# Attention's decay summed by a scan on VectorE instead of products with a triangle, and the convolution's first output ahead, in a two-layer hybrid trunk

## The chip, the cores and the metric

The kernel runs on one core of a Trainium2 chip. The metric is the device time of one execution in microseconds; the median of the runs stands for the kernel. Of an execution taken by the profiler there are also the span (first to last instruction) and a trace of every engine: TensorE (PE, its weight loads PEld), VectorE (DVE), ScalarE (ACT), GpSimd (POOL) and SyncE's queue of DMA issues (SPq).

## The reference

A trunk of two layers on 512 tokens of width 1024. Each layer has a SwiGLU feed-forward block (inner width 2816) at half weight, a mixer, and a second such block, each behind an RMSNorm. The mixer projects the normalised input once and splits the columns over three groups: a causal convolution of width 3, HGRN2 (a gated linear recurrence, 4 heads), and FoX, attention with a forget gate (8 heads). What the change touches is FoX's decay and the convolution:

```python
def short_conv_mixer(x_in, b_gate, c_gate, conv_w):
    u = c_gate * x_in
    ...                       # y = causal depthwise convolution of u, width 3
    return b_gate * y

def fox_mixer(q, k, v, f_logit, f_bias, q_gain, k_gain):
    ...
    log_f = jax.nn.log_sigmoid((f_logit + f_bias).astype(f32))
    cum = jnp.cumsum(log_f, axis=1).transpose(0, 2, 1)
    ...
        s = (jnp.einsum('bhqd,bhkd->bhqk', qb, kh).astype(f32)
             + (cb[..., :, None] - cum[..., None, :]))
        s = jnp.where(qpos[:, None] >= kpos[None, :], s, MASK_VALUE)
        p = jax.nn.softmax(s, axis=-1)
```

`cum` is the running sum of the gates' logarithms over the 512 tokens, for each of 8 heads.

## The kernel before, in words

Activations lie with features on the 128 partitions and the 512 tokens along the row. Almost all products are float32 split into a rounded part and a rest, three products for one (`mm3`, lines 496, 502 and 503, or line 582 where `stream_steps` writes the order of the rests out, `lows`). Weights come by DMA from SyncE's queue into a stage tile `st` (L417), ScalarE copies the rounded part into a tile `hl` (L477), and VectorE subtracts it to get the rest (L483). `stream_steps` goes through a projection in granules of `kk` blocks of 128 rows; a granule has a list `order` of (output bank, block), three products each. It is block by block, with the output banks in turn, except where `lead` is set in the first granule, or in the last granule: there it is bank by bank.

PSUM has eight banks with names that go round: three `mm`, two `sc`, two `pt`, one `po`.

In a mixer (`mix`) the order is this. First come HGRN's projections and the tokens' gates, the FoX forget logits `zf` among them (128 partitions x 4 blocks of tokens x 8 heads). Then two generators `run`, one for each pair of HGRN heads, are stepped beside `dense`, FoX's projections (`fox_qkv`: q and k of four heads twice, and the values, each with four output banks `mm`, `mm`, `mm`, `po`). HGRN's tensors of 128x512 are taken from a pool of ten tiles `t`. In a step of `run` the state is summed by a scan on VectorE (L1636), the operands of levels 0 and 1 are made (L1654 to L1659), and the scores of these levels are taken on TensorE (L1676); the operands of the later levels follow (L1665 to L1668) with their scores (L1686).

`fox_decay` is called between these steps, once in a layer, after the operands of levels 0 and 1. It makes the logarithms `lf` (128 x 4 x 8) and sums them over the tokens: it splits `lf` into a rounded part `lh` and a rest `ll` (L1803, L1804), and for each block j of 128 tokens multiplies both by `utri`, a constant of 128x512 whose first 128 columns are an upper triangle of ones and whose others are all ones (L1808, eight products of 512, 384, 256 and 128 columns). The sum stands in a `pt` bank as 8 heads x 512 tokens. ScalarE writes its negative, rounded, to `negc` (L1812), VectorE the rest (L1813), and SyncE sends both to device memory (L1818), from where the attention's preparation of each head reads them (L1904). The constant is built once in the opening (`build_consts`, L355 to L358).

After `dense` comes `conv`, run beside the attention's steps (`BESIDE`). It makes two projections of two outputs each (`features_steps`, granules of four blocks, `deep=4`), with output banks `mm`, and then a third. The banks that the first of them takes are those that held the values' projection, which ScalarE and VectorE clear (L1884, L1885).

Instructions are put in order on each engine by a planner with modelled durations, with the program's order as priority; chains written out by hand (`follow`, `keep`) fix the order of TensorE's products in `conv`, in attention and in `dense`.

Of the kernel before, what the change touches and what calls it, by code (L numbers as in the profile page):

```python
# [8 lines left out]
F32 = mybir.dt.float32  # L9
F32R = mybir.dt.float32r  # L10
# [3 lines left out]
AF = mybir.ActivationFunctionType  # L14
ALU = mybir.AluOpType
# [13 lines left out]
P = 128  # L29
T = 512  # L30
# [54 lines left out]
NH = 8  # L85
C_X, C_B, C_C, H_Q, H_F, H_I, H_G = (256 * i for i in range(7))
# [130 lines left out]
def halves(x):  # L217

    return x.rearrange("p (h t) -> p h t", h=2)


def unwoven(bank):

    return bank.rearrange("p (t h) -> p h t", h=2)
# [12 lines left out]
def inner(x):  # L237

    return x.rearrange("p (b t h) -> p b h t", h=2, t=CH)
# [12 lines left out]
class Trunk:  # L252
# [40 lines left out]
    def build_consts(self, scratch):  # L293

        nc = self.nc
        c = self.const

        self.ones_blk = c.tile([P, P], F32R, tag="ones_blk", name="ones_blk")
        nc.vector.memset(self.ones_blk.bitcast(F32), 0.0)
        for h in range(2):  # L300
            r = slice(64 * h, 64 * h + 64)
            nc.vector.memset(self.ones_blk[r, r].bitcast(F32), 1.0 / 64)

        self.heads2 = c.tile([P, 2], F32, tag="heads2", name="heads2")
        nc.vector.memset(self.heads2, 0.0)
        for h in range(2):
            nc.vector.memset(self.heads2[64 * h : 64 * h + 64, h : h + 1], 1.0)

        self.smask = c.tile([P, T], F32, tag="smask", name="smask")
        nc.vector.memset(self.smask, 1.0)  # L310
        nc.vector.memset(self.smask.rearrange("p (c t) -> p c t", t=CH)[:, :, 0:1], 0.0)
        self.identb = c.tile([P, P], BF16, tag="identb", name="identb")
        nc.vector.tensor_copy(self.identb, self.ident)
        self.utri = c.tile([P, T], F32R, tag="utri", name="utri")
        self.maskb = c.tile([P, P], BF16, tag="maskb", name="maskb")

        self.lmask = c.tile([P, 6, CH], U8, tag="lmask", name="lmask")
        self.same = c.tile([P, CH], F32, tag="same", name="same")
        ft = scratch(I32)[:, :P]
        pt = scratch(I32)[:, :P]  # L320
        nc.gpsimd.iota(ft, pattern=[[1, P]], base=0, channel_multiplier=0)
        nc.gpsimd.iota(pt, pattern=[[0, P]], base=0, channel_multiplier=1)
        ftf = scratch(F32)[:, :P]
        ptf = scratch(F32)[:, :P]
        x = scratch(I32)[:, :P]
        for i in (
            nc.vector.tensor_copy(ftf, ft), nc.vector.tensor_copy(ptf, pt),
            nc.vector.tensor_tensor(x, ft, pt, op=ALU.bitwise_xor),
        ):
            self.tc.add_manual_dep(i.ins, self.first_rows, NOSYNC, reason="opening order")  # L330
        xf = scratch(F32)[:, :CH]
        later = scratch(F32)[:, : P + CH]
        later, own = later[:, :P], later[:, P:]
        nc.vector.tensor_tensor(later, ftf, ptf, op=ALU.is_gt)
        for h in range(2):

            r = slice(CH * h, CH * h + CH)
            nc.vector.tensor_copy(xf[r], x[r, r])
            nc.vector.tensor_copy(own[r], later[r, r])
            nc.vector.tensor_copy(self.same[r], self.ident[r, r])  # L340
        a = scratch(F32)[:, :CH]
        b = scratch(F32)[:, :CH]
        for l in range(1, 7):
            nc.vector.tensor_scalar(
                a, xf, scalar1=float(2 ** (l - 1)), scalar2=None, op0=ALU.is_ge
            )
            nc.vector.tensor_scalar(b, xf, scalar1=float(2**l), scalar2=None, op0=ALU.is_lt)
            nc.vector.tensor_mul(a, a, b)
            nc.vector.tensor_mul(self.lmask[:, l - 1, :], a, own)

        nc.vector.tensor_scalar(
            inner(self.maskb)[:, 0], halves(later), scalar1=-1e30, scalar2=None, op0=ALU.mult
        )

        nc.vector.tensor_tensor(self.utri[:, :P], ftf, ptf, op=ALU.is_ge)  # L355
        of = scratch(F32)[:, P:]
        nc.vector.memset(of, 1.0)
        nc.vector.tensor_copy(self.utri[:, P:], of)  # L358

    def n(self, s):  # L360
        self.uid += 1
# [955 lines left out]
    def mix(self, l, w, w_out, conv_w, out_gain, q_gain, k_gain, f_bias, next_gain, logits):  # L1317
        nc, tc = self.nc, self.tc
        FM2 = [slice(0, P), slice(P, 2 * P)]
        TOK = [slice(c, c + P) for c in (0, 128, 256, 384)]  # L1320
        with tc.tile_pool(name=self.n("mix"), bufs=1) as mp:
# [23 lines left out]
            def features_steps(spans, banks, mid=None, **kw):  # L1345

                bs = [self.bank(t) for t in banks]
                yield from self.stream_steps(
                    [(b, c, None) for b, c in zip(bs, FM2)], cols(*spans), self.xact, KD, mid, **kw
                )  # L1350
                return bs
# [18 lines left out]
            with tc.tile_pool(name=self.n("hg"), bufs=1) as hp:  # L1370
# [3 lines left out]
                negc = mp.tile([NH, 2, T], F32R, tag="n", name=self.n("negc"))  # L1374
# [11 lines left out]
                for i in range(2):  # L1386
# [8 lines left out]
                    out=self.inv2, in0=self.invc, scalar=1.0 / HD, in1=self.invc,  # L1395
                    op0=ALU.mult, op1=ALU.mult,
# [12 lines left out]
                for i in range(4):  # L1409
                    nc.scalar.activation(  # L1410
                        halves(v[:, i, :]), unwoven(bv[i][:, :256]), AF.Copy,
                        scale=self.invc[:, i : i + 1],
                    )
                    nc.vector.scalar_tensor_tensor(
                        out=halves(zf[:, i, :]), in0=unwoven(bv[i][:, 256:264]),
                        scalar=self.invc[:, i : i + 1], in1=halves(fb), op0=ALU.mult, op1=ALU.add,
# [25 lines left out]
            with tc.tile_pool(name=self.n("at"), bufs=1) as ap_:  # L1442
# [7 lines left out]
                beside = dict(keep=True, fine=True, deep=4)  # L1450

                def conv():
                    inv2 = ap_.tile([P, T], F32, tag="t", name=self.n("iv2"), bufs=self.tb)
                    nc.scalar.activation(inv2, inv, AF.Square)
                    for i in range(2):
                        bx, bc = yield from features_steps(
                            [(C_X + i * P, P), (C_C + i * P, P)], ("mm", "mm"), **beside
                        )
                        self.conv_in(ap_, i, bx, bc, inv2, cw)
                    bb = yield from features_steps([(C_B, 256)], ("mm", "mm"), **beside)  # L1460
                    self.conv_out(ap_, 0, bb[0])
                    return bb[1]
# [32 lines left out]
                def rest():  # L1495
                    yield from dense
                    yield from most((yield from conv()))
# [10 lines left out]
                for dg in range(2):  # L1508
# [5 lines left out]
                    for i in range(4):  # L1514
                        j = 4 * dg + i
# [276 lines left out]
    def fox_decay(self, mp, hp, zf, negc):  # L1792

        nc = self.nc
        a = mp.tile([P, 4, NH], F32, tag="fa", name=self.n("fa"))
        lf = mp.tile([P, 4, NH], F32, tag="fl", name=self.n("fl"))
        nc.vector.scalar_tensor_tensor(out=a, in0=zf, scalar=-1.0, in1=zf, op0=ALU.mult, op1=ALU.min)
        self.act(a, a, AF.Exp)
        self.act(a, a, AF.Ln, bias=1.0)
        nc.vector.scalar_tensor_tensor(out=lf, in0=zf, scalar=0.0, in1=a, op0=ALU.min, op1=ALU.subtract)  # L1800
        lh = mp.tile([P, 4, NH], F32R, tag="flh", name=self.n("flh"))
        ll = mp.tile([P, 4, NH], F32R, tag="fll", name=self.n("fll"))
        nc.scalar.copy(lh, lf)  # L1803
        nc.vector.tensor_sub(ll, lf, lh)  # L1804
        cb = self.bank("pt")
        for j in range(4):
            for part in (lh, ll):
                nc.tensor.matmul(  # L1808
                    cb[:NH, j * P :], part[:, j, :], self.utri[:, : T - j * P],
                    start=j == 0 and part is lh, stop=j == 3 and part is ll,  # L1810
                )
        nc.scalar.activation(negc[:, 0, :], cb[:NH, :], AF.Copy, scale=-1.0)  # L1812
        nc.vector.scalar_tensor_tensor(  # L1813
            out=negc[:, 1, :], in0=cb[:NH, :], scalar=-1.0, in1=negc[:, 0, :],
            op0=ALU.mult, op1=ALU.subtract,
        )
        self.negc = self.dram.tile([NH, 2, T], F32, tag="negc", name=self.n("negc"))
        nc.sync.dma_start(self.negc, negc.bitcast(F32))  # L1818
# [389 lines left out]
```

## Time and profile before

| | before |
|---|---|
| median of 3 runs | 1737.31 us (1736.97 to 1737.51) |
| profiled execution, its time | 1737.04 us |
| its span | 1735.1 us |
| TensorE busy | 1730.3 us |
| VectorE busy | 1416.6 us |
| ScalarE busy | 1010.3 us |

The span goes from the first instruction to the last; the time of the execution is 1.9 us more. A matmul's end is modelled, so a row's start is the surer number: the distance from one start to the next tells what a product takes from TensorE in a full stream.

### The profile page before, as it was taken

Reading aid. Unit: us, or ns where it says so; the run is one execution under the profiler, and the core shown is the slowest. Engines: PE = TensorE matmul, PEld = TensorE weight load, DVE = VectorE, ACT = ScalarE, POOL = GpSimd, SP = SyncE. Lnnn points to the kernel's source line nnn. Section 1 sums busy time; section 2 is a strip of 40 time slices with the busy share of each in tenths; the row PEclk is TensorE's granted clock in tenths of the full one; section 3 lists DMA queues with packets and bytes.
Section 4 is the critical chain, followed back from the end, with each engine's and each line's share of the span. In section 5 each row is a group of like instructions: output and inputs, shape, how many; then the busy total and the mean of one; then the engine's idle time right before and its main releaser. Section 6 shows DMA issues by size and latency. Waiting matters only on the chain.

```text
span 1735.1 us, 32597 instructions
## 1 busy us (share of the span) xinstructions
PE 1730.3 (100%) x13215; PEld 1626.5 (94%) x13215; DVE 1416.6 (82%) x1926; ACT 1010.3 (58%) x1407; POOL 176.0 (10%) x174
## 2 busy tenths in 40 slices
PE   9999999999999999999999999999999999999999
PEld 8999999888888999999989999998888889999998
DVE  7988787778888898888688887876878879888884
ACT  5565665465766565566446556555667665655651
POOL 0011120100000112012001111201000000120110
PEclk9999999999999999999999999999999999999999
DMA  7768784243542966868276787933435438668672
GB/s 218 189 150 194 186 176 104 74 126 93 142 128 92 241 154 154 209 160 171 85 194 168 177 182 177 194 82 76 116 99 150 118 120 208 158 147 228 145 161 97
DMA packets 249766, 262.29 MB, mean 151 GB/s; under 512 B 25816, under 2 KB 221152, under 8 KB 249616
## 3 DMA queue, kind: packets, MB, share of 16 engines
q1 hardware_dynamic: 197344, 192.02, 37.1%
q0 software_dynamic: 52256, 68.19, 24.2%
q8 instruction: 104, 1.70, 0.4%
q14 instruction: 46, 0.38, 0.1%
q10 hardware_dynamic: 16, 0.00, 0.0%
HBM read 226.15 MB, written 2.17 MB: 132 GB/s over the span
## 4 chain that ended last, share of the span: by engine, by line
PE 99%; DMA 0%; DVE 0%; ACT 0%; SPq 0%; issue 0%
PE mm L496 11%; PE mm L502 11%; PE mm L503 11%; PE mm L582 9%; PE pt L496 7%; PE pt L503 7%; PE pt L502 7%; PE sc L496 6%; PE sc L502 6%; PE sc L503 6%; PE po L496 3%; PE po L502 3%; PE po L503 3%; PE po L582 2%; PE sc L1944 1%; PE po L2016 1%
## 5 line engine op out<-in xcount | busy, mean ns | idle before, releaser
L1040 DVE TENSOR_TENSOR hl<-w,hl 128x1024 fp32r<-128x1024 f32 x279 | 340.9, 1222 | 97.6 <-ACT hl L1036 95.8
L1036 ACT CAST hl<-w 128x1024 fp32r<-128x1024 f32 x279 | 292.3, 1048 | 207.3 <-PE pt L503 50.6
L483 DVE TENSOR_TENSOR hl<-st,hl 128x1024 fp32r<-128x1024 f32 (+3 forms) x152 | 160.0, 1055 | 95.2 <-ACT hl L477 94.0
L477 ACT CAST hl<-st 128x1024 fp32r<-128x1024 f32 (+3 forms) x151 | 137.4, 913 | 152.6 <-PE po L503 37.1
L496 PE MATMUL mm<-xc,hl 128*128 128x256 f32 x698 | 191.5, 275 | 0.0
L502 PE MATMUL mm<-xc,hl 128*128 128x256 f32 x696 | 191.5, 275 | 0.0
L503 PE MATMUL mm<-xc,hl 128*128 128x256 f32 x696 | 191.4, 275 | 0.0
L496 PE MATMUL pt<-xc,hl 128*128 128x256 f32 x546 | 150.1, 275 | 0.0
L502 PE MATMUL pt<-xc,hl 128*128 128x256 f32 x544 | 149.7, 275 | 0.0
L503 PE MATMUL pt<-xc,hl 128*128 128x256 f32 x544 | 149.6, 275 | 0.0
L496 PEld LDWEIGHTS mm<-xc,hl 128*128 128x128 f32 x698 | 133.9, 192 | 0.1
L502 PEld LDWEIGHTS mm<-xc,hl 128*128 128x128 f32 x696 | 133.6, 192 | 0.0
L503 PEld LDWEIGHTS mm<-xc,hl 128*128 128x128 f32 x696 | 133.6, 192 | 0.0
L496 PE MATMUL sc<-xc,hl 128*128 128x256 f32 (+1 forms) x466 | 127.9, 275 | 0.0
L502 PE MATMUL sc<-xc,hl 128*128 128x256 f32 x464 | 127.7, 275 | 0.0
L503 PE MATMUL sc<-xc,hl 128*128 128x256 f32 x464 | 127.6, 275 | 0.0
L582 PE MATMUL mm<-hl,x 128*128 128x512 f32 x432 | 107.4, 384 | 0.0
L496 PEld LDWEIGHTS pt<-xc,hl 128*128 128x128 f32 x546 | 104.6, 192 | 0.3
L502 PEld LDWEIGHTS pt<-xc,hl 128*128 128x128 f32 x544 | 104.4, 192 | 0.3
L503 PEld LDWEIGHTS pt<-xc,hl 128*128 128x128 f32 x544 | 104.4, 192 | 0.0
L496 PE MATMUL mm<-x,hl 128*128 128x512 f32 x272 | 103.6, 381 | 0.1
L503 PE MATMUL mm<-x,hl 128*128 128x512 f32 x272 | 103.1, 379 | 0.0
(542 smaller groups left out, 5309.3 us busy)
## 6 DMA issues: line engine op xcount, KB each, us to landing
w<-in_ffn_w_in_dram SPq DMA_DIRECT2D x124, 512.0 KB, 5.5
w<-in_ffn_w_out_dram POOLq DMA_DIRECT2D x50, 512.0 KB, 9.6
w<-in_ffn_w_out_dram SPq DMA_DIRECT2D x49, 512.0 KB, 4.6
st<-in_ffn_w_out_dram SPq DMA_DIRECT2D x39, 512.0 KB, 3.6
st<-in_w_mix_in_dram SPq DMA_DIRECT2D x72, 256.0 KB, 3.1
st<-in_ffn_w_in_dram SPq DMA_DIRECT2D x71, 256.0 KB, 3.3
w<-in_ffn_w_in_dram POOLq DMA_DIRECT2D x29, 512.0 KB, 9.3
w<-S POOLq DMA_DIRECT2D x29, 512.0 KB, 5.1
```

Source lines behind the costliest of these rows:

```text
L477: a = nc.scalar.copy(hi, src[:, c : c + w])
L483: b = nc.vector.tensor_sub(lo, src[:, c : c + w], hi)
L496: i = nc.tensor.matmul(acc[:, c], ah, bh[:, c.start // 2 : c.stop // 2, :], start=first and c.start == 0, stop=False, skip_group_check=True,)
L502: nc.tensor.matmul(acc, ah, bl, start=False, stop=False, skip_group_check=True)
L503: i = nc.tensor.matmul(acc, al, bh, start=False, stop=last, skip_group_check=True)
L582: self.follow("p", self.nc.tensor.matmul(acc, *((w, woven(x)) if toks is None else (x[:, toks], woven(w))), start=k == 0 and id(acc) not i ...
L1036: A(nc.scalar.copy(hi, src))
L1040: return lambda: V(nc.vector.tensor_sub(lo, src, hi))
L1944: mm = lambda *a, **k: E(nc.tensor.matmul(*a, skip_group_check=True, **k))
L2016: E(nc.tensor.matmul(self.ob[:, o * P : (o + len(at)) * P], half[2][:, j, h].rearrange("p a d -> p (a d)"), turned_in(part[:, at[0] : at[- ...
```

## The change

The constant `utri` goes, and a row of ones (a constant that is there already) is named instead. In `fox_decay` the split and the eight products go. TensorE turns the four blocks of `lf` (128x8 to 8x128) into one `pt` bank, and VectorE sums along the row of 512 with a scan into a tile `c`, from the pool of ten tiles `t`. The two writes of `negc` read `c` in SBUF instead of the bank. In `conv` the first of the two projections gets `lead`, so that the first granule goes bank by bank.

```diff
-        self.utri = c.tile([P, T], F32R, tag="utri", name="utri")
+        self.ones_row = nc.const_aps.tensor(1.0, [NH, T], F32)
...
-        nc.vector.tensor_tensor(self.utri[:, :P], ftf, ptf, op=ALU.is_ge)
-        of = scratch(F32)[:, P:]
-        nc.vector.memset(of, 1.0)
-        nc.vector.tensor_copy(self.utri[:, P:], of)
...
                         bx, bc = yield from features_steps(
-                            [(C_X + i * P, P), (C_C + i * P, P)], ("mm", "mm"), **beside
+                            [(C_X + i * P, P), (C_C + i * P, P)], ("mm", "mm"), lead=i == 0, **beside
                         )
...
-        lh = mp.tile([P, 4, NH], F32R, tag="flh", name=self.n("flh"))
-        ll = mp.tile([P, 4, NH], F32R, tag="fll", name=self.n("fll"))
-        nc.scalar.copy(lh, lf)
-        nc.vector.tensor_sub(ll, lf, lh)
         cb = self.bank("pt")
         for j in range(4):
-            for part in (lh, ll):
-                nc.tensor.matmul(
-                    cb[:NH, j * P :], part[:, j, :], self.utri[:, : T - j * P],
-                    start=j == 0 and part is lh, stop=j == 3 and part is ll,
-                )
-        nc.scalar.activation(negc[:, 0, :], cb[:NH, :], AF.Copy, scale=-1.0)
+            nc.tensor.transpose(cb[:NH, j * P : (j + 1) * P], lf[:, j, :], self.ident)
+        c = hp.tile([P, T], F32, tag="t", name=self.n("fc"), bufs=self.tb)[:NH, :]
+        nc.vector.tensor_tensor_scan(c, self.ones_row, cb[:NH, :], 0.0, op0=ALU.mult, op1=ALU.add)
+        nc.scalar.activation(negc[:, 0, :], c, AF.Copy, scale=-1.0)
         nc.vector.scalar_tensor_tensor(
-            out=negc[:, 1, :], in0=cb[:NH, :], scalar=-1.0, in1=negc[:, 0, :],
-            op0=ALU.mult, op1=ALU.subtract,
+            out=negc[:, 1, :], in0=c, scalar=-1.0, in1=negc[:, 0, :], op0=ALU.mult, op1=ALU.subtract
         )
```

## The prediction

> **What bounds the kernel now.** I read the page first (busy times, clock, chain), then TensorE's waits, then its timeline at the places that the change touches, then VectorE beside them.
>
> ```profile
> PE 1730.3 (100%) x13215; PEld 1626.5 (94%) x13215; DVE 1416.6 (82%) x1926; ACT 1010.3 (58%) x1407; POOL 176.0 (10%) x174
> ...
> PEclk9999999999999999999999999999999999999999
> ...
> PE 99%; DMA 0%; DVE 0%; ACT 0%; SPq 0%; issue 0%
> ...
> PE po L2130 <- PEq L2193: 0.8, 1, 0.8
> PE sc L550 <- ACT x L651: 0.3, 1, 0.3
> ```
>
> TensorE is busy all the span, at full clock, and is 99% of the chain that ended last. The last two rows are the whole answer on what TensorE waited for: 1.1 us, both in the opening. So an edit counts by what it takes out of TensorE's stream of starts, or by a stop that it brings into it. A busy TensorE can hide short stops, since the ends are modelled; those show only as a larger distance from one start to the next.
>
> **The decay on TensorE.** The first row below is the dense product ahead of the decay in layer 0, then come the first and the last two of its eight products and what follows; the last three rows are layer 1.
>
> ```profile
> 387.58 0.38 PE L582 MATMUL po<-hl,x 128*128 128x512 f32 x1
> 387.79 0.39 PE L1808 MATMUL pt<-utri,flh 128*8 128x512 f32 x1
> ...
> 388.82 0.22 PE L1808 MATMUL pt<-utri,flh 128*8 128x128 f32 x1
> 388.88 0.22 PE L1808 MATMUL pt<-utri,fll 128*8 128x128 f32 x1
> 389.04 2.03 PE L1676 MATMUL sc<-heads,t 128*64 128x2 f32 x64
> 391.00 3.72 PE L582 MATMUL mm<-hl,x 128*128 128x512 f32 x16
> ...
> 1247.54 0.39 PE L1808 MATMUL pt<-utri,flh 128*8 128x512 f32 x1
> ...
> 1248.64 0.22 PE L1808 MATMUL pt<-utri,fll 128*8 128x128 f32 x1
> 1248.79 2.03 PE L1676 MATMUL sc<-heads,t 128*64 128x2 f32 x64
> ```
>
> From the first start of the decay to the start of the next work is 389.04 - 387.79 = 1.25 us, and 1248.79 - 1247.54 = 1.25 us in layer 1. That is what the eight products take from a full TensorE. Four turns of a 128x8 tile replace them. No turn of this shape is in the trace; the nearest rows are HGRN's turns of 128x128, amid the same dense products:
>
> ```profile
> 375.26 0.60 PE L1603 MATMUL pt<-ident,t 128*128 128x128 f32 x4
> 375.62 1.54 PE L582 MATMUL mm<-hl,x 128*128 128x512 f32 x6
> ...
> L1603 PE MATMUL pt<-ident,t 128*128 128x128 f32 x8 | 1.2, 272 | 0.0
> ```
>
> One lasts 0.272 us, and four end 0.60 us after the first start, so they start (0.60 - 0.272) / 3 = 0.11 us apart. The next product starts 375.62 - 375.26 = 0.36 us after the first turn. The six products there take 1.54 us, where five starts 0.216 apart (the distance of 387.58 to 387.79) and one duration of 0.38 make 1.46: 0.08 us of slow start. So four turns cost 0.36 + 0.08 = 0.44 us. Lower bound: starts 0.06 us apart, as the two 128-column products on a weight of 8 columns (388.82, 388.88), 0.24 us. Upper bound: no overlap, 4 x 0.272 = 1.09 us. I take 0.44, since operation, type and length are those of L1603 and only the weight is narrower. Saving per layer 1.25 - 0.44 = 0.81 us (1.01 to 0.16); both layers 1.6 us (2.0 to 0.3).
>
> [...]
>
> **The convolution's first output ahead.** In the first granule (four blocks of rows) of its first projection, products went to the two banks in turn; now all twelve go to the first bank, then twelve to the second. The rows: TensorE in layer 0, then layer 1, and VectorE clearing the value projection's second bank.
>
> ```profile
> 448.03 0.38 PE L496 MATMUL mm<-x,hl 128*128 128x512 f32 x1
> 448.25 0.38 PE L502 MATMUL mm<-x,hl 128*128 128x512 f32 x1
> 448.46 0.38 PE L503 MATMUL mm<-x,hl 128*128 128x512 f32 x1
> 448.90 0.45 PE L496 MATMUL mm<-x,hl 128*128 128x512 f32 x1
> 449.19 0.38 PE L502 MATMUL mm<-x,hl 128*128 128x512 f32 x1
> ...
> 1308.21 0.38 PE L503 MATMUL mm<-x,hl 128*128 128x512 f32 x1
> 1308.65 0.46 PE L496 MATMUL mm<-x,hl 128*128 128x512 f32 x1
> 1308.94 0.38 PE L502 MATMUL mm<-x,hl 128*128 128x512 f32 x1
> ```
> ```profile
> 448.01 0.74 DVE L1885 SCALAR_TENSOR_TENSOR V<-mm,invc,V 128x512 fp32r<-128x512 f32 x1
> ...
> 449.27 0.74 DVE L1885 SCALAR_TENSOR_TENSOR V<-mm,invc,V 128x512 fp32r<-128x512 f32 x1
> ```
>
> The fourth product starts 0.44 us after the third, the fifth 0.29 us after the fourth, instead of 0.216 each: 0.29 us lost (layer 1: 0.44 + 0.29 - 0.43 = 0.30). The fourth is the first into the second bank, which VectorE leaves at 448.01 + 0.74 = 448.75. This is a stop that the waits don't list. After the change that bank is wanted twelve products later, at 448.03 + 12 x 0.216 = 450.6, 1.9 us after it is free, so the stop goes. What is late next: the third bank, free at 449.27 + 0.74 = 450.01, is wanted only in the next pair of projections, after 48 products or 10 us. Number of products, weights, loads and casts stay. Saving 0.6 us in both layers; bounds 0 and 0.6.
>
> **The scan and the small work.** Removed on ScalarE and VectorE are a copy (L1803) and a subtraction (L1804); added is a scan over 8x512 on VectorE; the two writes of negc now read its result from SBUF. The scan's nearest row has the same length on 128 rows; L1813 on 8 rows takes about what L1885 takes on 128, so I take the whole 1.22 us (lower bound L1813's 0.65).
>
> ```profile
> L1636 DVE TENSOR_TENSOR_SCAN S<-t,t x4: 1217/1218/1258, 384.3 to 1246.7; 128x512 f32<-128x512 f32 x4
> ...
> 385.92 0.69 DVE L1654 TENSOR_TENSOR t<-q,lk 128x512 f32<-128x512 f32 x1
> ...
> 388.73 0.46 DVE L1659 TENSOR_TENSOR t<-t,lk 128x256 f32<-128x256 f32 x1
> ...
> 393.09 0.65 DVE L1813 SCALAR_TENSOR_TENSOR negc<-pt,negc 8x512 fp32r<-8x512 f32 x1
> ...
> 394.27 0.41 DVE L1668 TENSOR_TENSOR t<-t,q 128x256 f32<-128x256 f32 x1
> ...
> 400.50 2.34 DVE L483 TENSOR_TENSOR hl<-st,hl 128x1024 fp32r<-128x1024 f32 x2
> ...
> 401.62 2.07 PE L1686 MATMUL pt<-t 64*64 64x32 f32 x128
> ...
> 403.62 1.56 PE L582 MATMUL mm<-hl,x 128*128 128x512 f32 x6
> ```
> ```profile
> 393.77 0.36 SPq L1818 DMA_DIRECT2D negc<-negc  x1
> 401.74 2.77 SPq L417 DMA_DIRECT2D st<-in_w_mix_in_dram  x3
> 405.48 0.25 SPq L1904 DMA_DIRECT2D kb<-negc  x1
> ```
> ```profile
> 388.00:396.00 8.00, 8.00 (x95) 6.89 (x94) 7.65 (x20) 5.51 (x10) 0.00 (x0) 1.00 0.27 62
> 396.00:405.00 9.00, 9.00 (x161) 7.70 (x160) 9.00 (x20) 6.68 (x11) 0.15 (x1) 1.00 0.21 59
> ```
>
> VectorE is full here (7.65 of 8, 9.00 of 9 us), so the scan pushes what stands behind it by about 1.2 us. Behind it are HGRN's operands for the next levels and the splits of the dense weights. I cost this at nothing, and the cover is this: the operands of levels 2 and 3 are complete with the L1668 that ends at 394.7, and TensorE reads them in L1686 at 401.6, 6.9 us later; of the two splits from 400.50 the first is done at 401.7, and the dense granule that reads it begins at 403.6, 1.9 us later. If that cover were gone, the cost is up to 1.2 us a layer. The write of negc goes out 1.2 us later, 395.0 for 393.8; on SyncE the next issue behind it is the weight load at 401.74, and its first reader is issued at 405.48: both hold 6 us. The scan's output takes one of the ten shared "t" tiles for about 2 us; the tiles of the state's scan (L1636) come free at 388, so I cost that at nothing, with the same 1.2 us as the price if it isn't so. In the opening three VectorE instructions for the triangle go (0.29, 0.38 and 0.36 us); TensorE's only wait there for another engine is on ScalarE (L651), so nothing; bounds 0 and 0.3 us gained.
>
> **Sum.** 1.6 + 0.6 = 2.2 us off the profiled execution: span 1735.1 to 1732.9, its time 1737.04 to 1734.8. The median shown is 0.27 us above that execution, so the forecast is 1737.31 - 2.2 = 1735.1 us, 0.13% less. By the bounds of the turns alone it is 1734.7 to 1736.4. I count less than 0.2% (3.5 us) as no change that a measurement can tell, so the forecast is "same".
>
> **Rivals.**
> 1. The scan delays TensorE at once. L1676's last quarter reads what L1659 writes until 388.73 + 0.46 = 389.19. It starts at 389.04 + 0.75 x 1.96 = 390.5, and after the change 0.8 earlier, 389.7: 0.5 us of slack. A scan placed ahead of L1659 on VectorE stops TensorE for 1.22 - 0.5 = 0.7 us a layer: 2.2 - 1.4 = 0.8 us gained, 1736.5 us. For it: turns end sooner, so the scan is ready sooner. Against: in program order L1659 stands ahead of the decay, and L1813 of the same function came 4 us after it.
> 2. Slower: the same scan, put further ahead, so that VectorE stands still for turns that TensorE has not reached. With turns at 387.8 to 388.2 the scan ends near 389.5, and if the work from 385.9 to 389.2 (3.3 us) stood behind it, L1659 would end near 392.8, 3.1 us after TensorE wants it. Less 1.1 us gained that is 2.0 us lost a layer, 1741.3 us. It decides from a stop of 2.85 us a layer (1.1 + 1.74). Against it the same 4 us of L1813.
> 3. It doesn't do what it says: turns at 0.27 us each and the second bank late by another clearing; 0.3 us gained, 1737.0 us. Against: the 0.11 us of L1603, and 1.9 us of room at the bank.
> 4. Faster by over 0.2%: the order of all engines' work here comes from a planner with modelled durations, and new ones may put it otherwise. A change between dense and HGRN products costs TensorE: the sixteen products at 391.00 take 3.72 us for 15 x 0.216 + 0.38 = 3.62, and L1676 starts 0.16 instead of 0.06 us after the last L1808, some 0.2 us for both ends. Beyond the forecast 1.3 us are wanted, six or seven such changes fewer; 1733.6 us. Nothing in the trace speaks for so many.
>
> **Chances.** Forecast 0.60, rival 1 0.13, rival 2 0.08, rival 3 0.10, rival 4 0.09. Forecast, 1 and 3 are within 0.2%: 0.83; faster 0.09, slower 0.08. The range runs from 1733.4 (forecast with the lower bound of the turns, a gain of 0.3 in the opening and a regrouping or two in each layer) to 1738.0 (rival 3 with a stop of some tenths of a microsecond in each layer and the spread of the runs).
>
> **What would show it.** Right: the decay's turns start 0.11 us apart, TensorE goes from dense product to L1676 in about 0.45 us, the convolution's starts stay 0.216 us apart past the third product, and the scan takes 1.2 us with TensorE's list of waits as short as now. Wrong: TensorE's starts spread at L1676 or L1686 with the scan just before on VectorE; turns 0.27 us apart; another order of the groups between 370 and 450 us; or a difference far from these places.

## The result, and the profile after

| | before | after |
|---|---|---|
| median, 21 runs each | 1737.70 us (1736.97 to 1739.33) | 1735.34 us (1734.72 to 1739.71) |
| profiled execution: its time, its span | 1737.04, 1735.1 us | 1735.9, 1734.0 us |

The ratio is 0.9987 (95% interval 0.9981 to 0.9992): about 2.3 us less (1.4 to 3.3 by the interval), which is within the 0.2% that I count as no change, though this many runs do tell it from nothing. The page after has the same picture as before: TensorE is the span and the chain, and its list of waits for other engines stays short. These are the page's row of busy times, its row of the chain by engine, and TensorE's two waits.

```profile
PE 1729.4 (100%) x13207; PEld 1627.2 (94%) x13207; DVE 1417.1 (82%) x1923; ACT 1010.2 (58%) x1405; POOL 175.9 (10%) x174
...
PE 99%; DVE 1%; issue 0%; ACT 0%; ACTq 0%
...
PE po L2118 <- PEq L2181: 0.8, 1, 0.8
PE po L491 <- DVE u L1211: 0.2, 1, 0.2
```

The lines of the kernel after are 5 to 12 lower than before: L491, L497 and L498 are the three products of `mm3` (before L496, L502, L503), L577 is `stream_steps`' (before L582), L1798 the turns, L1800 the scan, L1671 and L1681 HGRN's scores (before L1676 and L1686), L1859 the clearing of `qk` (before L1871).

This is TensorE's timeline after: the decay in layer 0, the dense projection behind it and at its second half, the start of the convolution in layer 0, then the decay in layer 1. Columns: start, length, engine, line, operation, tiles, shape, count of equal rows in a stretch.

```profile
388.58 0.38 PE L577 MATMUL po<-hl,x 128*128 128x512 f32 x1
388.80 0.60 PE L1798 MATMUL pt<-ident,fl 128*8 128x128 f32 x4
389.33 2.03 PE L1671 MATMUL sc<-heads,t 128*64 128x2 f32 x64
391.29 3.72 PE L577 MATMUL mm<-hl,x 128*128 128x512 f32 x16
...
396.57 3.62 PE L577 MATMUL mm<-hl,x 128*128 128x512 f32 x16
...
448.68 0.38 PE L498 MATMUL mm<-x,hl 128*128 128x512 f32 x1
448.89 0.38 PE L491 MATMUL mm<-x,hl 128*128 128x512 f32 x1
449.11 0.38 PE L497 MATMUL mm<-x,hl 128*128 128x512 f32 x1
...
1247.46 0.60 PE L1798 MATMUL pt<-ident,fl 128*8 128x128 f32 x4
1247.99 2.04 PE L1671 MATMUL sc<-heads,t 128*64 128x2 f32 x64
```

Three things are to be seen.

- The four turns last 0.60 us from the first start, as L1603's did, so they start 0.11 us apart. From the first turn to L1671 it is 389.33 - 388.80 = 0.53 us, and 1247.99 - 1247.46 = 0.53 in layer 1, where the eight products took 1.25. That is 0.72 us off in each layer.
- The convolution's fourth product starts 0.21 us after the third, and the fifth 0.22 after the fourth. The stop of 0.29 us is gone; in layer 1 it is gone too, 0.30 us.
- Sixteen dense products at 396.57 take 3.62 us, which is 15 x 0.216 + 0.38. Before, they took 3.68 there:

```profile
396.28 3.68 PE L582 MATMUL mm<-hl,x 128*128 128x512 f32 x16
...
398.22 0.57 ACT L1871 COPY qk<-mm 128x512 f32<-128x512 f32 x1
```

The products from 396.28 open a third bank "mm" amid the stretch, and that bank was cleared only by the ScalarE copy from 398.22 to 398.79; the weight load behind it, at 398.83, had stood 0.20 us for that copy. After the change ScalarE has that copy ahead, at 396.34:

```profile
396.34 0.58 ACT L1859 COPY qk<-mm 128x512 f32<-128x512 f32 x1
```

So a stop of 0.07 us went at 399 us, and by the same comparison of starts 0.11 us at 1258 us. I had not forecast it. The sum of the starts, layer by layer, is 0.72 + 0.72 + 0.29 + 0.30 + 0.07 + 0.11 = 2.2 us. The profiled execution shows 1.1 us less span, not 2.2, because it has a loss of its own in the opening: by 88 us it is 1.0 us behind, in code that is the same in the kernel with the decay alone, whose execution is not behind. The product at that place, before, after (with its short wait), and in the decay alone (experiment 1):

```profile
87.47 0.35 PE L496 MATMUL po<-xc,hl 128*128 128x256 f32 x1
```
```profile
88.47 0.35 PE L491 MATMUL po<-xc,hl 128*128 128x256 f32 x1 [0.24 <-DVE u L1211]
```
```profile
87.42 0.28 PE L491 MATMUL po<-xc,hl 128*128 128x256 f32 x1
```

VectorE, beside the decay after: it takes the scan at once, behind L1654, whose result L1671 reads, and ahead of the later levels' operands (L1660, L1661).

```profile
389.51 0.43 DVE L1654 TENSOR_TENSOR t<-t,lk 128x256 f32<-128x256 f32 x1
389.85 1.20 DVE L1800 TENSOR_TENSOR_SCAN fc<-const-float32-1.0,pt 8x512 f32<-8x512 f32 x1
390.98 0.39 DVE L1660 TENSOR_TENSOR t<-kb,b 128x256 f32<-128x256 f32 x1
...
400.90 0.41 DVE L1663 TENSOR_TENSOR t<-t,q 128x256 f32<-128x256 f32 x1
```

### The profile page after: what moved, and what is told of

Same layout as the page of the kernel before. It is cut to its first block, busy times and chain, and to the rows that moved or that the text cites. A ratio compares the mean times of both kernels' runs of the same rounds, so it can differ in the third digit from the quotient of the medians.

```text
span 1734.0 us, 32580 instructions
## 1 busy us (share of the span) xinstructions
PE 1729.4 (100%) x13207; PEld 1627.2 (94%) x13207; DVE 1417.1 (82%) x1923; ACT 1010.2 (58%) x1405; POOL 175.9 (10%) x174
## 4 chain that ended last, share of the span: by engine, by line
PE 99%; DVE 1%; issue 0%; ACT 0%; ACTq 0%
PE mm L491 11%; PE mm L497 11%; PE mm L498 11%; PE mm L577 9%; PE pt L497 7%; PE pt L491 7%; PE pt L498 7%; PE sc L497 6%; PE sc L491 6%; PE sc L498 6%; PE po L491 3%; PE po L497 3%; PE po L498 3%; PE po L577 2%; PE sc L1932 1%; PE po L2004 1%
## 5 line engine op out<-in xcount | busy, mean ns | idle before, releaser
L491 PE MATMUL mm<-xc,hl 128*128 128x256 f32 x698 | 191.7, 275 | 0.0
L497 PE MATMUL mm<-xc,hl 128*128 128x256 f32 x696 | 191.6, 275 | 0.0
L498 PE MATMUL mm<-xc,hl 128*128 128x256 f32 x696 | 191.6, 275 | 0.0
L491 PE MATMUL pt<-xc,hl 128*128 128x256 f32 x546 | 150.1, 276 | 0.0
L497 PE MATMUL pt<-xc,hl 128*128 128x256 f32 x544 | 149.8, 275 | 0.0
L498 PE MATMUL pt<-xc,hl 128*128 128x256 f32 x544 | 149.6, 275 | 0.0
L491 PEld LDWEIGHTS mm<-xc,hl 128*128 128x128 f32 x698 | 133.9, 192 | 0.2 <-ACT u L1208 0.2
L498 PEld LDWEIGHTS mm<-xc,hl 128*128 128x128 f32 x696 | 133.6, 192 | 0.1
L497 PEld LDWEIGHTS mm<-xc,hl 128*128 128x128 f32 x696 | 133.6, 192 | 0.0
L491 PE MATMUL sc<-xc,hl 128*128 128x256 f32 (+1 forms) x466 | 128.0, 275 | 0.0
L497 PE MATMUL sc<-xc,hl 128*128 128x256 f32 x464 | 127.7, 275 | 0.0
L498 PE MATMUL sc<-xc,hl 128*128 128x256 f32 x464 | 127.6, 275 | 0.0
L577 PE MATMUL mm<-hl,x 128*128 128x512 f32 x432 | 107.2, 384 | 0.0
L491 PEld LDWEIGHTS pt<-xc,hl 128*128 128x128 f32 x546 | 104.7, 192 | 0.3
L497 PEld LDWEIGHTS pt<-xc,hl 128*128 128x128 f32 x544 | 104.4, 192 | 0.3
L498 PEld LDWEIGHTS pt<-xc,hl 128*128 128x128 f32 x544 | 104.5, 192 | 0.0
L491 PE MATMUL mm<-x,hl 128*128 128x512 f32 x272 | 103.4, 381 | 0.0
L498 PE MATMUL mm<-x,hl 128*128 128x512 f32 x272 | 103.1, 379 | 0.0
```

What stands on the lines that cost most here:

```text
L491: i = nc.tensor.matmul(acc[:, c], ah, bh[:, c.start // 2 : c.stop // 2, :], start=first and c.start == 0, stop=False, skip_group_check=True,)
L497: nc.tensor.matmul(acc, ah, bl, start=False, stop=False, skip_group_check=True)
L498: i = nc.tensor.matmul(acc, al, bh, start=False, stop=last, skip_group_check=True)
L577: self.follow("p", self.nc.tensor.matmul(acc, *((w, woven(x)) if toks is None else (x[:, toks], woven(w))), start=k == 0 and id(acc) not i ...
```

## The experiments

The main theory is the prediction's: the time is what the changed instructions take from TensorE's full stream of starts, and VectorE's scan is covered. Its rivals: the turns cost their whole length, so that their number is dear; the scan on VectorE is what counts, through a stop of TensorE; and, from experiment 2 on, TensorE's clock moves the runs as well, outside the changed lines. Each expectation says for itself which theory stands for what in that run. The edits shown are shortened. "Before" is the kernel before, run on the same chip beside each.

**1 and 2: each part alone.**

```diff
# e1: after, without the convolution's part
-   ("mm", "mm"), lead=i == 0, **beside
+   ("mm", "mm"), **beside
# e2: before, with that part alone
-   ("mm", "mm"), **beside
+   ("mm", "mm"), lead=i == 0, **beside
```

> The changed kernel without the convolution's lead: the decay's turns and scan alone. Theory (two independent savings on TensorE, 0.7 us a layer by the turns, 0.3 us a layer by the lead): 1.4 us faster than before, and the two stops of 0.29 us at the convolution's fourth product are back. Rival (the whole gain is a new order made by the planner, and the turns' own saving is taken back by the scan): the time stays within 0.5 us of before, or TensorE's groups between 370 and 450 us come in another order.

> The kernel before with the convolution's lead alone. Theory: 0.6 us faster than before, the starts of the convolution's first products 0.216 us apart in both layers, nothing else moved. Rival (the stop moves to the next bank or granule): the fourth product is on time but a stop of 0.2 us or more stands within the next 48 products, and the time is that of before.

Decay alone: 1735.64 us beside 1737.58, ratio 0.9985 (0.9976 to 0.9993). Lead alone: 1736.70, ratio 0.9992 (0.9983 to 1.0001); by the time alone that is not told from no change, so the lead's part rests on the starts. In the starts the parts stand apart and add up: the decay alone has 0.72 and 0.71 us at the decay, 0.07 and 0.11 at the third bank, and the convolution's stop is back:

```profile
447.51 0.38 PE L498 MATMUL mm<-x,hl 128*128 128x512 f32 x1
447.95 0.46 PE L491 MATMUL mm<-x,hl 128*128 128x512 f32 x1
448.25 0.38 PE L497 MATMUL mm<-x,hl 128*128 128x512 f32 x1
```

The lead alone has 0.29 and 0.30 us at the convolution and nothing elsewhere in the starts. But its profiled execution is longer than the one before, and the reason is a stretch that the edit does not touch. TensorE's timeline of e2 in layer 1, then the windows across it (the column behind the POOL numbers is the granted clock):

```profile
1248.45 2.03 PE L1676 MATMUL sc<-heads,t 128*64 128x2 f32 x64
1250.41 5.41 PE L582 MATMUL mm<-hl,x 128*128 128x512 f32 x16
```
```profile
1249.00:1250.50 1.50, 1.50 (x53) 1.48 (x49) 1.15 (x4) 1.50 (x3) 0.00 (x0) 1.00 0.34 80
1251.00:1253.50 2.50, 2.50 (x8) 1.96 (x7) 2.50 (x7) 1.64 (x3) 0.00 (x0) 0.50 0.30 72
1254.50:1255.50 1.00, 1.00 (x7) 0.87 (x6) 1.00 (x4) 0.94 (x2) 0.00 (x0) 1.00 0.00 0
```

The granted clock drops to 0.50 from 1250.60 to 1254.01, a stretch of 3.41 us (its mean is 0.80 from 1250 to 1251 and 0.66 from 1253 to 1254.5), right behind the two-column products of L1676 (64 rows; the trace has two rows for each of these 32 float32 products), and the sixteen dense products take 5.41 us for 3.72: 1.7 us. The page's clock row shows nines alone here too, since a slice of it is 43 us long and a nine stands for 90% or more. I come back to it at experiments 6 to 12.

**3: five times the turns.** On after, each turn is made five times over; the last one stands.

```diff
+   for _ in range(5):
        nc.tensor.transpose(cb[:NH, j * P : (j + 1) * P], lf[:, j, :], self.ident)
```

> The changed kernel with each of the decay's turns written five times into the same place, so 16 turns more in each layer; the result is that of one. Theory (a turn takes its distance from start to start, 0.11 us): 16 x 0.109 = 1.74 us a layer, 3.5 us slower than the changed kernel, so about 1.1 us slower than before. [...]

1738.49 us, ratio 1.0002 (0.9993 to 1.0011). By starts it is 1.74 us more than after in each layer. The rows are TensorE's, its weight load's (PEld) and VectorE's, then the window with the clock:

```profile
388.19 2.35 PE L1799 MATMUL pt<-ident,fl 128*8 128x128 f32 x20
390.46 2.03 PE L1671 MATMUL sc<-heads,t 128*64 128x2 f32 x64
```
```profile
390.46 1.95 PEld L1671 LDWEIGHTS sc<-heads,t 128*64 128x64 f32 x64 [0.22 <-issue]
```
```profile
390.57 1.21 DVE L1801 TENSOR_TENSOR_SCAN fc<-const-float32-1.0,pt 8x512 f32<-8x512 f32 x1 [1.19 <-PE pt L1799]
```
```profile
390.00:393.00 3.00, 3.00 (x72) 2.67 (x71) 2.32 (x4) 1.63 (x3) 0.00 (x0) 1.00 0.34 82
```

Sixteen turns more cost 16 x 0.109 = 1.74 us; at their whole length of 0.272 us they would have cost 4.4. That rival is out: here a turn took 0.11 us from a full stream. The granted clock stays at 1.00 behind the 20 turns in a row (2.3 us), and in none of the 11 executions was its mean below 1.00.

Two more things are in these rows. From the last turn's start (388.19 + 19 x 0.109 = 390.26) to L1671 it is 0.20 us, as in the kernel after. There the trace puts the 0.22 us that L1671's weight load stood down to VectorE's scan of the state (L1631), which ends just before; here that scan had ended at 388.60, and the 0.22 us are the same, with nothing to wait for. So it is the way out of the turns and not a wait. And VectorE stood 1.19 us for the turns, with the later operands behind the scan, which is the mechanism of rival 2; L1654 had ended before, and TensorE shows no stop.

**4: five times the scan.** On after, the scan is made five times, 4.8 us more of VectorE in each layer.

```diff
+   for _ in range(5):
        nc.vector.tensor_tensor_scan(c, self.ones_row, cb[:NH, :], 0.0, op0=ALU.mult, op1=ALU.add)
```

> The changed kernel with the scan made five times into the same tile, 4 x 1.20 = 4.8 us more on VectorE in each layer. If the cover of VectorE is the 1.9 us that the prediction named (first split done 1.9 us ahead of the dense granule): TensorE stops 2.9 us a layer, 5.8 us slower than the changed kernel. If the cover is what the changed kernel's trace shows for the next scores (operands complete at 396.9, read at 401.85: 4.9 us) and for the rest of the weights (written at 399.8, read at 405.6: 5.8 us): no stop, or under 0.2 us a layer, and a time within 0.5 us of the changed kernel. If VectorE bounds this stretch: 4.8 us a layer, 9.6 us slower.

1742.61 us, ratio 1.0029 (1.0020 to 1.0038). TensorE now waits for VectorE, by its list of waits and its timeline in layer 0:

```profile
PE pt L1681 <- DVE t L1663: 4.0, 4, 1.3
```
```profile
401.48 0.67 PE L1681 MATMUL pt<-t 64*64 64x32 f32 x32
402.85 1.14 PE L1681 MATMUL pt<-t 64*64 64x32 f32 x64 [0.70 <-DVE t L1663]
405.28 0.67 PE L1681 MATMUL pt<-t 64*64 64x32 f32 x32 [1.29 <-DVE t L1663]
405.87 2.93 PE L577 MATMUL mm<-hl,x 128*128 128x512 f32 x6
```

The 128 rows of L1681 take 405.87 - 401.48 = 4.39 us for 2.00 after (401.85 to 403.85): 2.4 us of stop. None of the three sizes that I had expected (2.9, none, 4.8 us) is that. The scan pushes the operands of the next scores, as the prediction had it, but the cover behind the scan that is there is 4.8 - 2.4 = 2.4 us, not the longer one that I had counted.

The rows show why. The scores come in four quarters of 32 rows and each quarter reads one L1663. In the kernel before, the fourth of these (L1668 there) ended at 394.7. After the change VectorE has it at 400.90, ending at 401.31, behind the weights' splits; its quarter starts at 401.85 + 0.75 x 2.00 = 403.35. That leaves 2.0 us, close to the 2.4 measured; the two need not be equal, since VectorE's order is another one in 4. The scan's own 1.2 us were free, and some 2.0 to 2.4 us more would have been.

In both layers together the stops make 4.8 us. The other 1.9 us of the profiled execution (1742.05 less the median after, 1735.34, and less 4.8) are in the main a fall of the clock right behind the stop in layer 0 (0.50 from 405.85 to 409.26, by means of 0.92 from 405 to 406 and 0.87 from 409 to 410: six products in 2.93 us, where after they would take 5 x 0.216 + 0.38); the mean clock was below 1.00 in all 11 executions. The scan's rival holds as a mechanism with the scan five times over, and not for this scan; by the cover of 2.4 us I estimate that it begins at about three times this scan's length (1.2 + 2.4 us).

**5: the decay a step earlier.** On after, `fox_decay` is called ahead of the step of `run`, so that the turns have more time before their first reader.

```diff
+   if step == 0:
+       self.fox_decay(mp, hp, zf, negc)
    for g in run + run: next(g)
-   if step == 0:
-       self.fox_decay(mp, hp, zf, negc)
```

> The changed kernel with the decay called one step earlier in the program, ahead of the operands of levels 0 and 1. Rival 1 of the prediction (a scan ahead of L1659's place on VectorE stops TensorE at the scores of levels 0 and 1): a wait of about 0.7 us a layer on VectorE at that group, 1.4 us slower than the changed kernel. Cover as wide there as at the later scores (2.4 us, from the scan made five times): no wait, and if the turns then stand ahead of a dense product instead of the scores, their way out is 0.11 us instead of 0.20, 0.1 us a layer faster.

1737.92 us beside 1737.35, ratio 1.0000 (0.9991 to 1.0009): the whole gain is lost. By starts it is 1.3 us in each layer at a place that neither theory named, the state's products L1620 (64 rows):

```profile
381.70 0.60 PE L1798 MATMUL pt<-ident,fl 128*8 128x128 f32 x4
382.24 1.02 PE L1620 MATMUL pt<-v,t 64*64 64x64 f32 x26
383.61 1.15 PE L1620 MATMUL pt<-v,t 64*64 64x64 f32 x38 [0.35 <-DVE fc L1800]
384.68 1.56 PE L577 MATMUL mm<-hl,x 128*128 128x512 f32 x6
```

These rows take 384.68 - 382.24 = 2.44 us, where before they take 1.09 from first start to the dense product behind (TensorE's rows before):

```profile
381.42 1.16 PE L1625 MATMUL pt<-v,t 64*64 64x64 f32 x64
382.51 1.56 PE L582 MATMUL mm<-hl,x 128*128 128x512 f32 x6
```

They write two "pt" banks, and one of these the scan must leave first; the wait that is shown is 0.35 us a time, and the rest is starts further apart. The scan holds its bank for 1.2 us, which does no harm where the next taker of "pt" is far, as in the changed kernel, and does here.

**6 and 8: what the triangle costs.** On before: the eight products three times over, and the triangle's decay called early as in 5.

```diff
# e6
-   for j in range(4):
+   for j in list(range(4)) * 3:
# e8: on before, the two lines moved as in experiment 5
```

> The kernel before with the eight products by the triangle made three times into the same place (the last time counts), 2 x 1.25 = 2.5 us a layer more on TensorE. Theory A (products on a weight of 8 columns and the 64 small products behind them let TensorE's clock fall, and their length together decides): the stretch is 3.75 + 1.96 = 5.7 us long, the granted clock is 0.5 behind it in both layers of nearly every execution, some 1.7 us each, and the time is 5.0 + 3.4 = 8.4 us above before, 1746 us. Theory B (the falls come with the 64 small products alone): 5.0 us above before, 1742.6 us, with the same share of executions 1.7 us longer as before has, about a third.

> The kernel before with the decay called one step earlier in the program, so that the triangle's products no longer stand right ahead of the 64 small products. Theory A (their length together decides on the fall of the clock): executions that are 1.6 us longer become rare, at most one in ten, as with the changed kernel, and the median falls by 0.3 us or so towards the lower group of before, 1737.1. Theory B (the small products alone): about a third of the executions stays 1.6 us longer.

e6 has 1744.52 us (1742.54 to 1746.10), ratio 1.0037 (1.0025 to 1.0050). Its starts give 1.17 us for each further eight products; the rows are the first product of the first eight and of the third:

```profile
388.27 0.39 PE L1808 MATMUL pt<-utri,flh 128*8 128x512 f32 x1
...
390.62 0.39 PE L1808 MATMUL pt<-utri,flh 128*8 128x512 f32 x1
```

That is the prediction's 1.25 less the way out to L1676, which is paid once. The clock fell in 3 of its 5 executions, not in all, and the profiled one has no fall; the expectation that 2.3 us more of such products bring it down every time fell. The two executions without a fall are 5.2 and 5.6 us above before, of which the starts explain 4.7; the rest is open. e8 has 1740.46 us, ratio 1.0018 (1.0009 to 1.0027): the planner puts the state's products in two groups with dense ones between, 1.6 us a layer. Together with 5 it says that the decay's place is worth more than its instructions. In none of e8's 11 executions was the mean clock below 1.00, though the small products of L1676 are there as before, without the triangle right ahead of them. Three of these 11 are still 1.3 to 1.6 us above the median, so not every long execution is a fall.

**7 and 10: one turn for four.** On after: one turn of 128x32, one product with a column of ones for what comes ahead of each block, a scan of 128 on 32 rows instead of 512 on 8; in 10 the product is put ahead of the turn.

```diff
-   for j in range(4):
-       nc.tensor.transpose(cb[:NH, j * P : (j + 1) * P], lf[:, j, :], self.ident)
+   # before[:, j] = lf[:, 0] + ... + lf[:, j - 1], on VectorE
+   nc.tensor.transpose(cb[: 4 * NH, :P], flat(lf), self.ident)
+   nc.tensor.matmul(cb[: 4 * NH, P : P + 2], flat(before), self.ones_col, start=True, stop=True)
...
-   nc.vector.tensor_tensor_scan(c, self.ones_row, cb[:NH, :], 0.0, op0=ALU.mult, op1=ALU.add)
+   nc.vector.tensor_tensor_scan(c, self.ones_row, cb[: 4 * NH, :P], first[:, 0:1], op0=ALU.mult, op1=ALU.add)
```

> The changed kernel with one turn of 128x32 (4 blocks x 8 heads) instead of four of 128x8, a scan of 128 on 32 rows instead of 512 on 8, and the sums of earlier blocks as the scan's first value, by one product of two columns. Theory (what TensorE gives to the decay is turns at 0.11 us each and a way out of 0.20): 0.11 + 0.05 + 0.20 = 0.36 us a layer for 0.53, so 0.2 us a layer, 0.3 to 0.4 us faster than the changed kernel, and a scan of some 0.4 us for 1.20. Rival (four more small instructions on VectorE and the finer transfers to device memory cost as much): the same time as the changed kernel or above, with a wait on TensorE that was not there.

> The kernel with one turn, with the product of two columns put ahead of the turn instead of behind it, so that the turn stands right ahead of the small products. Theory (the length of the stretch without large products decides, 2.2 us with the product between turn and small products, 2.06 us without): falls as rare as with the changed kernel, the median 0.3 to 0.4 us below the changed kernel, about 1735.0 us. Rival (fewer turns, or the product itself, cause the falls): two in three layers fall as before, a median near 1737.9 us.

e7: 1737.91 us beside 1737.35, ratio 0.9999 (0.9990 to 1.0008); e10: 1736.89 beside 1737.40, ratio 0.9994 (0.9985 to 1.0003). Both gain less than the changed kernel (0.9987), though the intervals overlap a little, and though the decay itself is shorter (by 0.18 us a layer in 7, 0.07 in 10). In e7:

```profile
388.69 0.27 PE L1804 MATMUL pt<-ident,fl 128*32 128x128 f32 x1
388.89 0.22 PE L1805 MATMUL pt<-const-float32-1.0,flb 128*32 128x2 f32 x2
389.04 2.03 PE L1672 MATMUL sc<-heads,t 128*64 128x2 f32 x64
391.01 5.41 PE L578 MATMUL mm<-hl,x 128*128 128x512 f32 x16
```

The sixteen dense products behind the small ones take 5.41 us again. In e7 the mean clock was below 1.00 in 10 of 11 executions, in e10 in 8 of 11; in the kernel after in 1 of 21. The order of turn and product did not cure it, which I had expected of 10.

**9, 11 and 12: which work lets the clock fall.** On after, four more small products, 72 rows for 64 (9); on before, the group parted by two wide products whose result nothing reads (11); on 10, the small products on weights of 128 columns, half as many, of two columns each (12).

```diff
# e9
-   for c in range(NCH):
+   for c in [0, 1][: 2 * (lev == 0)] + list(range(NCH)):
# e11
+   if lev == 0 and pr == 1:
+       for _ in range(2):
+           nc.tensor.matmul(sb[0][:, 128:], self.none[:, :P], self.none[:, :128], start=True, stop=True)
# e12
+   for i in range(4):
+       matmul(sb[0][:, 8*at+i : 8*at+8 : 4], e[:, i*P:(i+1)*P], heads2)
```

> The changed kernel with two products of level 0 made twice for each pair of heads, which lengthens the group of 64 small products by 8, 0.24 us a layer; the result is the same. Theory (TensorE's clock falls for 3.4 us when a stretch of small products is longer than about 2.1 us, and 2.06 us, as in the kernel before and the changed one, lies at the edge): 0.5 us by the products themselves and a fall in half of the layers or more, 1.6 us each, so a median 2 us or more above the changed kernel, 1737.2 us or more. Rival (the many falls with one turn come from that kernel's own product on 32 columns or from fewer turns): 0.5 us above the changed kernel, 1735.8 us, and falls as rare as there, two in 21 executions.

> The kernel before with two products of 128 columns by a constant, which nothing reads, in the middle of the 64 small products of each layer. Theory (length of the stretch): two stretches of 1 us, no fall in any execution, all within 0.6 us of each other, near 1737.1 + 0.4 us for the products and their ways in and out. Rival (falls come with the small products however they lie): a third of the executions is 1.6 us longer, as before.

> The kernel with one turn and its carry ahead, and the small products of levels 0 and 1 made on 128 tokens at a time instead of 64, so 16 products of two columns in the place of 32 with the same result. A 128-column weight in float32 has its starts 0.109 us apart (the turns), so 16 take 1.74 us for 1.96: 0.2 us a layer. Theory (the length of the stretch of small products decides on the falls of the clock; it is now shorter than in the kernel before): no fall in any execution, a median 0.3 + 0.4 us below the changed kernel, about 1734.5 us. Rival (the falls follow the one turn, or small products however long they take): two in three layers fall as with one turn, a median near 1737 us.

e9: 1738.91 us beside 1737.40, ratio 1.0005 (0.9996 to 1.0014). The four products more cost 0.24 us a layer, and the clock fell in 11 of 11 executions:

```profile
1248.51 2.27 PE L1671 MATMUL sc<-heads,t 128*64 128x2 f32 x72
1250.71 5.41 PE L577 MATMUL mm<-hl,x 128*128 128x512 f32 x16
```

e11: 1737.67 us, ratio 1.0002 (0.9993 to 1.0011). The two wide products cost 0.32 us a layer (392.04 - 389.76 = 2.28 us for 1.96), and the clock still fell, in 2 of 11 executions. The profiled one is such:

```profile
389.76 1.10 PE L1679 MATMUL sc<-heads,t 128*64 128x2 f32 x32
390.79 0.29 PE L1676 MATMUL sc<-const-bfloat16-1.0 128*128 128x128 bf16 x2
391.01 1.10 PE L1679 MATMUL sc<-heads,t 128*64 128x2 f32 x32
392.04 4.47 PE L582 MATMUL mm<-hl,x 128*128 128x512 f32 x12
```

So the clock fell without an unbroken stretch of small products too. e12: 1744.29 us (1740.00 to 1744.93), ratio 1.0039 (1.0025 to 1.0053); the sixteen wide ones run as 32 records in 3.5 us, two each, which I had left out of the count, so from the decay's start to the dense products it is 1.4 us a layer more than with the narrow ones, and the clock fell in 4 of 5 executions. Few and wide was no cure either. No version ran faster than the changed kernel by more than the intervals tell.

## Why the prediction was right, point by point

- **The bound.** TensorE's starts are the time: 2.2 us by starts, 2.2 us forecast, 2.36 us between the medians of 21 runs. The median came at 1735.34 for 1735.1; that forecast started from the 1737.31 of 3 runs, where 21 runs of the kernel before have 1737.70, so the gain is the fairer comparison.
- **The decay.** The eight products' 1.25 us hold (1.17 and the way out in 6), and the turns start 0.11 us apart, as L1603 said. The term that was mis-sized is the way from the last turn to the next work: 389.33 less the last turn's start (388.80 + 3 x 0.109) is 0.20 us, where L1603's neighbours gave 0.11 with the slow start. Four turns cost 0.53 for 0.44 us, and the saving is 0.72 for 0.81 a layer. What is behind the turns differs: there it was a dense product, here a two-column product, and in 7 the way from a turn to another two-column product is 0.20 us too (388.69 to 388.89).
- **Full clock.** The page's clock row is no evidence of it: in experiment 2 that row is nines with a fall of 3.41 us in it. What shows it for the profiled execution before is the mean granted clock of 1.000 (0.999 in experiment 2).
- **The convolution.** 0.29 and 0.30 us, as forecast, with nothing late next.
- **VectorE.** The scan is covered, as forecast, but the cover named was not the one that counted. I took 6.9 us from the order of the trace before; VectorE's order changed with the scan, and 2.0 us were left by rows, 2.4 by experiment 4. The other cover named, 1.9 us at the dense granule, was not what ended the stop in 4.
- **Not forecast:** 0.07 and 0.11 us at the third bank, by another order on ScalarE. It made up for the turns' 0.09 a layer, so the sum fits better than its terms.
- **Rival 1** did not come: the scan stands right behind L1654 (before L1659), as its program order said. **Rival 2**'s mechanism, VectorE standing for turns that TensorE has not finished, did not come in the changed kernel; it came in 3 (1.19 us a layer) and in 5 (0.73 us ahead of the scan in layer 0), and TensorE did not stop at the scores of levels 0 and 1 for it. What stopped TensorE in 5 was the bank. **Rival 3** is out by 3, and **rival 4**'s regrouping didn't come in the changed kernel, though 5 and 8 show that a regrouping of the state's products is worth 1.3 to 1.6 us a layer, far more than the 0.2 at which I priced one.

## What to carry to other kernels

Where one engine is busy all the span, price an edit by the distances between starts and not by lengths: four turns of 0.27 us cost 0.53 together, and the way out to other work is a term of its own. A cover read from the trace before holds only as long as the planner keeps its order; look for the last reader of the last operand, quarter by quarter. And compare the granted clock over many executions, since a shorter piece of code can come with a stretch at half clock that costs more than it saves: in 7 the decay is 0.18 us a layer shorter, the clock fell in 10 of 11 executions, and the sixteen dense products in such a stretch took 1.7 us more.

## What the hardware showed that I had not expected

TensorE's granted clock fell to 0.50 right behind the 32 two-column products (64 rows, 1.96 us), in a stream without stops, for one stretch of 3.41 us in 2; in 9 it was 3.4 us (means of 0.58 from 1251 to 1252, 0.50 from there to 1254, 0.71 from 1254 to 1255). The sixteen dense products behind took 5.41 us for 3.72 in 2, 7, 9 and 10, which is 1.7 us more each time. The fall came in some executions of a kernel and not in others, and the share differs between kernels. The share of executions with a mean clock below 1.00:

| kernel | what is ahead of or in the small products | executions |
|---|---|---|
| before, run beside the experiments | triangle ahead | 17 of 95 |
| 2, 11 | triangle ahead; 11: group parted | 4 of 11, 2 of 11 |
| 6 | triangle three times ahead | 3 of 5 |
| 8 | triangle elsewhere | 0 of 11 |
| after, 1, 3 | four or twenty turns ahead | 1 of 21, 0 of 11, 0 of 11 |
| 4 | four turns ahead; a stop of TensorE later | 11 of 11 (in the profiled one, behind the stop) |
| 5 | turns elsewhere | 0 of 11 |
| 7, 10 | one turn and a two-column product ahead | 10 of 11, 8 of 11 |
| 9 | four turns ahead, 36 small products for 32 | 11 of 11 |
| 12 | one turn ahead, wide weights, 3.5 us | 4 of 5 |

The share was 11 of 11 with four more small products (9) and 1 of 21 without them (after). It was 10 and 8 of 11 with one turn and a two-column product ahead (7, 10), and 3 of 5 with the triangle three times ahead (6), for 17 of 95 with it once (before). The length of turns and group together does not order the kernels: in 3 it is 392.43 - 388.19 = 4.2 us and no execution fell, in 9 it is 1250.71 - 1247.98 = 2.7 us and all 11 did. What decides on a fall no run shows: 11 fell twice with wide products amid the group, and the kernel after fell once with nothing but turns ahead.

It also bears on the result. By these shares the change makes falls rarer, from 17 of 95 to 1 of 21 (few to tell by, but 1 of 43 with experiments 1 and 3, which have turns ahead as well), worth some (0.18 - 0.05) x 1.7 = 0.2 us in the mean of many executions. That is an estimate, and none of it is in the 2.2 us of the starts.
